# Two-layer hybrid encoder trunk: layer 2's first scale and shift loaded behind layer 1's experts, one more spare place, first copies reordered

## Chip, cores and metric

The kernel runs on one core of one Trainium2 chip. The metric is device time in microseconds (us) for one execution; lower is better. "Layer 1" is the first layer (index 0 in the code), "layer 2" the second (index 1).

## What is computed

256 tokens of width 1024 pass through two layers. Each layer is a mixer (layer 1: forgetting attention, layer 2: latent attention on keys and values that are computed once, between the layers) and a mixture of 16 experts with top-2 routing inside one group. Every sub-layer begins with an RMS norm and a shift and scale that come from a condition vector c, and ends with a gain from c:

```python
c_act = jax.nn.silu(c)
for layer in range(DEPTH):
    sh1, sc1, g1, sh2, sc2, g2 = jnp.split(c_act @ w_mod[layer] + b_mod[layer], 6, axis=-1)
    h = modulate(rmsnorm(x, norm_g), sh1, sc1)
    ...
    x = x + g1[:, None, :] * mix
    h = modulate(rmsnorm(x, ffn_norm_g[layer]), sh2, sc2)
    x = x + g2[:, None, :] * grouped_moe(h, ...)
    if layer == 0:
        shared_kv = mla_shared_kv(x, c_act, kv_norm_g, kv_w_mod, kv_b_mod, kv_w_down, ...)
return rmsnorm(x, final_norm_g)
```

All is float32. Every weight is read once from HBM, some 294 MB in all. `c_act @ w_mod` is a product of one row with a 1024 x 1024 block for each of the scales, shifts and gains: 4 MB to load, little to compute.

## The kernel before

**The stream of loads.** `plan` lists all weight loads in one order (lines 175 to 243), and SyncE's queue (SP) issues them in it as places come free, as far as the planner of the tile framework does not put one whose place is free ahead of one whose place is not. Most places are the ring `wp`: `NB` = 10 tiles of 1 MB. During the experts some loads go to spare places instead, made of tiles that lie idle then (`SPARE`, `SPAT`: the n-th entry of `SPAT[l]` names the expert load that goes to the n-th entry of `SPARE[l]`). `places` gives each later expert load the place of an earlier one. `give` opens a spare place, `drop` frees the place of the load at the head of the stream, `done` drops and then calls `mods`.

**Scales, shifts, gains.** They are entries `("mod", name, j)` of the same stream, four loads of 1 MB each (for the first scale and shift of layer 1 two halves of two loads, names in `HALVES`). `mods` (L323) works off those at the head of the stream. A name in `ONPE` is done on TensorE (L343): the column of c_act, spread to 32 columns, times the load, four products side by side. Any other name is done on VectorE (L349, L351): eight products over 128x1024 that add up in a tile `macc`, closed by short products with ones (L470). `finish_at[name]` then turns the row into columns: a copy out of PSUM (L476), a 4 KB DMA on GpSimd's queue (L482), and the bias and norm gain on VectorE (L483, L485); or, for a gain, spreads it over the partitions (L507, L509).

**Order of the instructions.** The planner of the tile framework orders each engine's instructions ahead of time, by its own idea of when operands and loads arrive; on the chip each engine then works strictly in that order. `tc.issue_after(i)` keeps what it encloses behind instruction `i` on `i`'s engine. `hold` names entries that `mods` leaves alone until they are released; `later` puts products behind a given instruction.

**Stages.** (1) Layer 1's input: norm, transposes, and the first group's products in two halves of the width (`turn_half`, `half_qk`, `half_v`, `half_f`). A weight is split on ScalarE and on VectorE or GpSimd into a high and a low part (`split`, L543, L544), and each product is three products (`mm3`, L548 to L550). (2) Attention over four groups of heads, then the output weight `a_w_o`. (3) `moe(0)`: router, routing on VectorE, gather of the tokens into 64 slots per expert (`fetch`, L895), then eight pairs of experts: gate and up products (`wide`, L925), down products (L1050), scatter products (L940, for the last pair L1076). Scale and shift of the attention between the layers (`sc_kv`, `sh_kv`) and layer 2's `sc1_1`, `sh1_1` are loaded ahead of the experts, the gain `g2_0` behind the first four expert loads. `sc1_1` is done on VectorE during the output weight, `sh1_1` on TensorE behind the router's products (L791 to L794). (4) `turn` (L574): norm, transposes (L583) and two sets of scaled parts (`leave`: L597, L603, L605, L606), `hk` for the keys and values with `sc_kv`, `sh_kv`, and `h2` for the queries with `sc1_1`, `sh1_1`; then products of `hk` with `kv_w_down` (`kvd`) and of `h2` with `b_w_dq` (`dq`). Layer 2's gain `g1_1` comes next in the stream and is done on VectorE. (5) Attention and output weight of layer 2, (6) `moe(1)`, (7) final norm.

Of the kernel before, what the change touches and what calls it, by code (L numbers as in the profile page):

```python
# [22 lines left out]
F32 = mybir.dt.float32  # L23
# [7 lines left out]
D = 1024  # L31
# [13 lines left out]
NEG = -1.0e30  # L45
NB = 10
HALVES = ('sc1_0a', 'sh1_0a', 'sc1_0b', 'sh1_0b')
ONPE = HALVES + ('sc2_0', 'sh_kv', 'sh1_1', 'g2_0', 'sc2_1', 'g2_1')
MB = 6
MP = (4, 0, 0, 0, 1, 1, 2, 1, 1, 2, 0, 0, 0, 0)  # L50
QA = (1, 0)
# [3 lines left out]
G2IN = 0  # L55
GAT = 4
LO = {'wf': 'V', 'wo0': 'VP', 'wo1': 'PVVV', 'in': 'PPPV', 'inv': 'P', 'kvd': 'VVPVPVPV', 'dq': 'PPVP', 'kvu': 'PV', 'uqr': 'VP', 'uq': 'P'}
SPAT = ((8, 9, 10, 11, 12, 13, 14), (3, 4, 5, 9, 10, 11, 12, 13, 14, 15))
KVF = 1
PVAT = 1  # L60
ORD = (1, 1, 0, 1, 2, 3)
# [13 lines left out]
def trunk_kernel(ctx, tc, A, out):  # L75
# [10 lines left out]
    def bank(i):  # L86
        return psp.tile([128, 512], F32, name=f"b{i}", tag=f"b{i}")
# [35 lines left out]
    class Pieces:  # L123
# [11 lines left out]
        def __getitem__(self, at):  # L135
            t, c = self.at[at[1]]
            return t[at[0], c + (at[2].start or 0):c + (at[2].stop or 512)]

    SPARE = {0: (("ka",) * 2, ("o8",), ("at",) * 4, ("at", "at", "v", "v"), ("wl",) * 4, ("wh",) * 4, ("x",)),
             1: (("yb", "yb", "g2"), ("macc",) * 2, ("ka",) * 2, ("o8",), ("at",) * 4, ("at", "at", "v", "v"), ("wl",) * 4,  # L140
                 ("g1", "ckvT"), ("wh",) * 4, ("x",))}
    AGAIN = (("at",) * 4, ("at", "at", "v", "v"), ("macc",) * 2, ("wl",) * 4, ("wh",) * 4, ("ka",) * 2)
# [50 lines left out]
    def in_half(j, c):  # L193
        return ("in", 0, j, c), win[:, 4 * c:4 * c + 4, j * D:j * D + 256]

    scb, shb = mod_half("sc1_0b", D + D // 2), mod_half("sh1_0b", D // 2)
    for it in (mod_half("sc1_0a", D) + mod_half("sh1_0a", 0)
               + [in_half(0, 0), scb[0], in_half(1, 0), scb[1], shb[0], in_half(2, 0), shb[1], (("wf", 0), wff[:, 0:4]),
                  (("wf", 1), wff[:, 4:8])]):
        plan(*it)  # L200
    main = [in_half(j, 1) for j in range(3)]
# [3 lines left out]
    wo = A["a_w_o"][0].rearrange("(k p) n -> p k n", p=128)  # L205
    for j in range(4):
        plan(("wo0", j), wo[:, 2 * j:2 * j + 2, :])
    side = (mod_unit("sc_kv", KVM, D) + mod_unit("sh_kv", KVM, 0)
            + mod_unit("sc1_1", W1, D) + mod_unit("sh1_1", W1, 0))
    for it in side:  # L210
        plan(*it)
    plan_moe(0, mod_unit("g2_0", W0, 5 * D))
    r = A["kv_w_down"].rearrange("(p k) n -> p k n", k=8)
    for j in range(2):
        plan(("kvd", j), r[:, 4 * j:4 * j + 4, :])
# [30 lines left out]
    state = {"issued": 0, "used": 0, "held": 0}  # L246
    macc = {}
    spare = []
    hold = {"sh1_1"}

    def issue():
        while state["issued"] < len(stream):
# [60 lines left out]
                            A["pack"][64 * c:64 * c + 64, ga0:ga0 + 8].rearrange("(q a) k -> q a k", a=16))  # L313

    def later(name, j):
        if name not in ("g2_0", "g2_1") or G2IN:
            return ExitStack()
        return behind(ORD[2 + j] if j < 4 else j)
# [4 lines left out]
    def mods():  # L323
        while state["used"] < len(stream) and stream[state["used"]][0][0] == "mod":
            key = stream[state["used"]][0]
            if key[1] in hold:
                return
            _, name, j = key
            w = get(key)
            if j == 0:  # L330
                macc[name] = bank(MB)[:, 0:128 if name in HALVES else 256] if name in ONPE else big.tile([128, D], F32, name="macc", bufs=2)
                if name in brows:
                    l, i = brows[name]
                    nc.gpsimd.dma_start(bcast[0:128:32, :],
                                        A["b_mod"][l, i * D:i * D + D].rearrange("(q n) -> q n", q=4))
            acc = macc[name]
            nk, n = (4, 128) if name in HALVES else (2, 256)
            for kk in range(nk):
                k = nk * j + kk
                if name in ONPE:  # L340
                    with later(name, j):
                        for q in range(4):
                            PE.matmul(acc[32 * q:32 * q + 32, :], cact[:, k:k + 1].to_broadcast([128, 32]),  # L343
                                      w[:, kk, n * q:n * q + n], start=k == 0, stop=k == 7)
                else:
                    at = state.get("rope") or state.get("turned")
                    with tc.issue_after(at) if at else ExitStack():
                        if k == 0:
                            V.tensor_scalar(acc, w[:, kk, :], cact[:, 0:1], None, op0=ALU.mult)  # L349
                        else:  # L350
                            V.scalar_tensor_tensor(acc, w[:, kk, :], cact[:, k:k + 1], acc,  # L351
                                                   op0=ALU.mult, op1=ALU.add)
            drop()
            if k == 7:
                if name in finish_at:
                    with later(name, 4):
                        finish_at.pop(name)()
# [216 lines left out]
    def turn(src, stride, nk, outs, banks):  # L574


        pss = {}
        for kk in range(0, nk, 2):
            ps = bank(banks[(kk // 2) % len(banks)])
            for k in (kk, kk + 1):  # L580
                for t in range(T):
                    o = (k - kk) * 256 + t * 128
                    PE.transpose(ps[:, o:o + 128], src[:, t, k::stride], ident)  # L583
            pss[kk] = ps.rearrange("p (a b) -> p a b", a=2)
            if len(outs) == 1:
                leave(pss, kk, *outs[0])
        if len(outs) > 1:
            for o in outs:
                for kk in range(0, nk, 2):
                    leave(pss, kk, *o)  # L590

    def leave(pss, kk, dst, G, sh, pair):
# [9 lines left out]
            else:  # L602
                SC.activation(hf[:, i], psv[:, i], AF.Identity, scale=G[:, k:k + 1], bias=sh[:, k:k + 1])  # L603
        if pair:
            SC.activation(d_[:, 0], hf, AF.Copy)  # L605
            at = (PL if kk % 4 else V).tensor_tensor(d_[:, 1], hf, d_[:, 0].bitcast(F32), op=ALU.subtract).ins  # L606
            if kk % 4 == 0:
                state["left"] = at
# [164 lines left out]
    def moe(l, G, sh, acc):  # L773
# [4 lines left out]
        for t in range(T):  # L778
            for c in range(2):
# [8 lines left out]
                for kk in range(4):  # L788
                    after[1] = PE.matmul(z[t], xT[:, kk, :], rwG[:, 4 * c + kk, :],
                                         start=c == 0 and kk == 0, stop=c == 1 and kk == 3).ins  # L790
        if hold:  # L791
            hold.clear()
            with tc.issue_after(after[1]):
                mods()  # L794
        give(l, "wh")
        rs = [rstd(slice(t, t + 1))[t] for t in range(T)]
        zz = wk.tile([128, T, E], F32, name="rzz", bufs=1)
# [207 lines left out]
        for i in range(E // 2):  # L1005
# [38 lines left out]
            for p, (c0, n) in enumerate(cols):  # L1044
# [3 lines left out]
                for k in range(4):  # L1048
                    for e in range(2):
                        at = PE.matmul(py[64 * e:64 * e + 64, 0:n], aT[:, k, 64 * e:64 * e + 64], ws[e][:, k, :],  # L1050
                                       start=k == 0, stop=k == 3).ins
                if i == OV - 1 and p == 1:
                    with tc.issue_after(at):
                        tc.mark_branch_hint_location(f"over{l}", "LikelyTaken", [mybir.EngineType.PE])
# [15 lines left out]
                if i == E // 2 - 1:  # L1070
# [2 lines left out]
                        x.new()  # L1073
                    for t in range(T):
                        for j, (pt, y_) in enumerate(parts_):
                            PE.matmul(acc[t, half][:, o:o + n], pt[:, t, :], y_, start=False,  # L1076
                                      stop=o + n == 512 and j == len(parts_) - 1)
                        if o + n == 512:
                            ch = slice(512 * half, 512 * half + 512)
                            if l == 0:  # L1080
# [1 line left out]
                            squares(t, half, None, acc[t, half])  # L1082
                    if l and o + n == 512:
                        gains(half, acc)


    for c, nm in enumerate("ab"):
# [65 lines left out]

    turn_half(0)
    half_qk(0, 0)
    half_qk(1, 0)
    half_v(0)
    half_f(0)
    turn_half(1)
    state["turned"] = state["left"]  # L1160
    half_f(1)
# [63 lines left out]
    xn = normalise()  # L1225
    hk = [big.tile([128, 2, 2, S], F32R, name="hk", tag=("qa", "ka")[i % 2], bufs=2) for i in range(4)]
    h2, h2p = parts("h2")
    turn(xn, 8, 8, [(hk, M["sc_kv"], M["sh_kv"], True), (h2p, M["sc1_1"], M["sh1_1"], True)], (0, 1, 2, 3))

    def rms_small(srcs, n, dst):  # L1230
        sq = sm.tile([128, len(srcs)], F32, name="sq")
# [247 lines left out]
```

## Time and profile before

| | us |
|---|---|
| three runs | 850.89, 847.19, 845.97 (median 847.19) |
| the profiled execution | 847.37 |
| its span, first to last instruction | 845.2 |
| TensorE (PE) busy | 759.6 (90%) |
| VectorE (DVE) busy | 374.7 (44%) |
| ScalarE (ACT) busy | 265.5 (31%) |
| GpSimd (POOL) busy | 169.5 (20%) |
| HBM | 294.32 MB read, mean 351 GB/s |

Busy times are of one profiled execution; the rows of a view count from the start of its span. Weight loads of TensorE (PEld) overlap its products, and the ends of products are modelled. A wait is put down to what ended it. In a timeline, the bracket behind a row tells how long the engine stood before it and what released it.

### The profile page before, as it was taken

What the parts mean: (1) busy time and instruction counts of PE and PEld (TensorE: products, weight loads), DVE (VectorE), ACT (ScalarE), POOL (GpSimd) and SP (SyncE); (2) the same over time, 40 slices, a digit from 0 to 9 for tenths busy, and PEclk for the clock granted to TensorE, in tenths of its full rate; (3) what the DMA queues carried; (4) which work ended last, traced back from release to release, by engine and by line L of the source; (5) the groups of instructions that cost most, each with busy time, mean ns of one, the idle gap of its engine ahead of it and who ended that gap; (6) DMA issues with size and microseconds to landing.
All of it is one profiled execution on the core that took longest, in us unless ns stands there. A gap on an engine that the chain in (4) does not pass through costs nothing.

```text
span 845.2 us, 11973 instructions
## 1 busy us (share of the span) xinstructions
PE 759.6 (90%) x4530; PEld 454.3 (54%) x4530; DVE 374.7 (44%) x838; ACT 265.5 (31%) x576; POOL 169.5 (20%) x155
## 2 busy tenths in 40 slices
PE   4788999988999999899886899899799999999985
PEld 3678789656335454343335677777544544445322
DVE  2279699876113211211128949865712311223112
ACT  2345556534111110110116565766411201111002
POOL 3446376321000000000005846421100000000000
PEclk9799999999999999999998999999799999999998
DMA  9999788799999999999998678977879999999993
GB/s 320 372 378 351 250 326 297 287 382 390 412 399 394 414 403 405 415 405 405 418 401 309 202 275 313 348 248 244 304 262 396 395 373 418 388 390 401 396 405 134
DMA packets 105960, 296.35 MB, mean 351 GB/s; under 512 B 8164, under 2 KB 27804, under 8 KB 93600
## 3 DMA queue, kind: packets, MB, share of 16 engines
q1 hardware_dynamic: 104976, 293.79, 92.0%
q10 hardware_dynamic: 288, 1.05, 0.3%
q8 instruction: 39, 0.64, 0.3%
q0 software_dynamic: 624, 0.60, 0.3%
q14 instruction: 33, 0.27, 0.1%
HBM read 294.32 MB, written 1.05 MB: 349 GB/s over the span
## 4 chain that ended last, share of the span: by engine, by line
issue 22%; PE 21%; DVE 8%; DMA 8%; ACT 2%; SPq 0%; POOLq 0%; POOL 0%; another core or an unknown queue 0%; ACTq 0%; DVEq 0%
DMA w<-in_exp_w_up_dram 7%; PE b L925 5%; PE b L1050 3%; PE b L548 2%; DVE macc L351 2%; PE b L549 2%; PE b L550 2%; PE b L895 1%; DVE wl L544 1%; DMA fg<-in_final_norm_g_dram 1%; PE b L940 1%; PE b L657 1%; PE b L343 1%; PE b L643 1%; PE b L619 1%
## 5 line engine op out<-in xcount | busy, mean ns | idle before, releaser
L925 PE MATMUL b<-w,XG 128*64 128x512 f32 x1024 | 234.3, 595 | 15.5 <-DMA w<-in_exp_w_up_dram 6.9
L544 POOL TENSOR_TENSOR wl<-w,wh 128x512 fp32r<-128x512 f32 (+3 forms) x90 | 132.8, 1490 | 331.8 <-DMA w<-in_b_w_dq_dram 218.3
L925 PEld LDWEIGHTS b<-w,XG 128*64 128x64 f32 x1024 | 80.7, 137 | 156.1 <-issue 125.5
L1050 PE MATMUL b<-w,aT 128*64 128x512 f32 (+1 forms) x528 | 121.8, 586 | 4.0 <-ACT aT L1038 4.0
L1025 DVE SCALAR_TENSOR_TENSOR act<-sg,rcs,b 128x512 f32<-128x512 f32 x16 | 12.0, 748 | 204.2 <-PE b L925 178.4
L543 ACT ACTIVATE wh<-w 128x512 fp32r<-128x512 f32 (+3 forms) x136 | 77.2, 588 | 80.0 <-PE b L549 28.8
L1050 PEld LDWEIGHTS b<-w,aT 128*64 128x64 f32 x528 | 39.4, 136 | 63.2 <-issue 51.3
L351 DVE SCALAR_TENSOR_TENSOR macc<-w,cact,macc 128x1024 f32<-128x1024 f32 x42 | 68.6, 1633 | 0.4
L1065 ACT ACTIVATE yh<-yb 128x512 fp32r<-128x512 f32 x31 | 19.5, 630 | 102.7 <-DVE yb L1063 102.7
L544 DVE TENSOR_TENSOR wl<-w,wh 128x512 fp32r<-128x512 f32 (+2 forms) x46 | 39.4, 864 | 20.4 <-ACT wh L543 20.3
L1063 DVE TENSOR_TENSOR yb<-b,g 128x512 f32<-128x512 f32 (+1 forms) x33 | 22.2, 674 | 58.5 <-PE b L1050 57.1
L565 POOL TENSOR_TENSOR rs<-rs,mhalf 128x1 f32<-128x1 f32 (+1 forms) x9 | 5.9, 652 | 199.4 <-DVE rs L564 199.3
L343 PE MATMUL b<-w,cact 128*32 128x256 f32 (+1 forms) x640 | 40.0, 368 | 6.2 <-DMA w<-in_w_mod_dram 6.0
L1014 ACT ACTIVATE sg<-b 128x512 f32<-128x512 f32 x16 | 9.6, 597 | 113.3 <-PE b L925 113.3
L1038 ACT ACTIVATE aT<-b 128x256 f32<-128x256 f32 x16 | 6.1, 384 | 124.1 <-PE b L1035 124.1
L895 PEld LDWEIGHTS b<-P,xs 128*128 128x128 f32 x256 | 35.9, 211 | 16.0 <-DVE XG L901 8.9
L548 PE MATMUL b<-h,wh 128*128 128x256 f32 (+1 forms) x136 | 41.1, 307 | 3.0 <-ACT h L605 2.2
L550 PE MATMUL b<-h,wl 128*128 128x256 f32 (+1 forms) x136 | 41.4, 306 | 1.2 <-POOL wl L544 0.9
L895 PE MATMUL b<-P,xs 128*128 128x256 f32 x256 | 40.9, 312 | 1.6 <-DVE P L860 1.6
L549 PE MATMUL b<-h,wh 128*128 128x256 f32 (+1 forms) x136 | 40.9, 302 | 0.0
L901 DVE TENSOR_SCALAR XG<-b,c_sc,c_sh 128x256 f32<-128x256 f32 x32 | 17.4, 543 | 36.6 <-ACT XG L903 36.4
L903 ACT ACTIVATE XG<-b,c_sh,c_sc 128x256 f32<-128x256 f32 x32 | 17.9, 560 | 46.9 <-PE b L895 46.9
(310 smaller groups left out, 1237.0 us busy)
## 6 DMA issues: line engine op xcount, KB each, us to landing
w<-in_exp_w_down_dram SPq DMA_DIRECT2D x50, 1024.0 KB, 14.8
w<-in_w_mod_dram SPq DMA_DIRECT2D x48, 1024.0 KB, 9.7
w<-in_exp_w_gate_dram SPq DMA_DIRECT2D x48, 1024.0 KB, 14.0
w<-in_exp_w_up_dram SPq DMA_DIRECT2D x48, 1024.0 KB, 15.1
w<-in_exp_w_gate_dram SPq DMA_DIRECT2D x42, 256.0 KB, 8.3
w<-in_exp_w_up_dram SPq DMA_DIRECT2D x40, 256.0 KB, 6.6
w<-in_a_w_in_dram SPq DMA_DIRECT2D x9, 1024.0 KB, 12.0
w<-in_kv_w_mod_dram SPq DMA_DIRECT2D x8, 1024.0 KB, 6.5
```

Of the source, the lines that this page charges most:

```text
L343: PE.matmul(acc[32 * q:32 * q + 32, :], cact[:, k:k + 1].to_broadcast([128, 32]), w[:, kk, n * q:n * q + n], start=k == 0, stop=k == 7)
L351: V.scalar_tensor_tensor(acc, w[:, kk, :], cact[:, k:k + 1], acc, op0=ALU.mult, op1=ALU.add)
L543: SC.activation(hi, src, AF.Copy)
L544: lo_eng.tensor_tensor(lo, src, hi.bitcast(F32), op=ALU.subtract)
L548: PE.matmul(ps, l[0], r_[0], start=start, stop=False)
L549: PE.matmul(ps, l[0], r_[1], start=False, stop=False)
L550: PE.matmul(ps, l[1], r_[0], start=False, stop=stop)
L895: at = PE.matmul(ps[:, 256 * kk:256 * kk + 256], xs[n % 2, n // 2][:, 128 * k:128 * k + 128], P[g][:, n // 2].rearrange("p e s -> p (e s)" ...
L925: last = PE.matmul(ps[64 * e:64 * e + 64, :], XG[i // 2, k // 4][:, k % 4, o:o + 64], ws[e][:, kk, :], start=k == 0, stop=k == 7).ins
L1050: at = PE.matmul(py[64 * e:64 * e + 64, 0:n], aT[:, k, 64 * e:64 * e + 64], ws[e][:, k, :], start=k == 0, stop=k == 3).ins
L1063: V.tensor_tensor(yb[:, 0:n], py[:, 0:n], M[f"g2_{l}"][:, cs_], op=ALU.mult)
L1065: SC.activation(yh[:, 0, cs_], yb, AF.Copy)
```

## The change

Four things change. `sc1_1` is done on TensorE, in PSUM bank 4. The eight loads of `sc1_1` and `sh1_1` stand behind all expert loads of layer 1 instead of ahead of them, and their products are placed by `later`: the first half of the scale behind the last down product of the layer, its second half and the shift's first load behind the last scatter product, the rest of the shift behind the last transpose of `turn`, which now works off what is held before it scales. The spare place (`ckvT`, `g2`) takes expert load 3 of layer 1. At the start, two halves of the scale and one of the shift are loaded ahead of the second input weight, the last half of the shift ahead of the third, and the second and third weights' work is kept behind ScalarE's last high part of the first half and behind the products of the shift's halves.

```diff
-ONPE = HALVES + ('sc2_0', 'sh_kv', 'sh1_1', 'g2_0', 'sc2_1', 'g2_1')
+ONPE = HALVES + ('sc1_1', 'sc2_0', 'sh_kv', 'sh1_1', 'g2_0', 'sc2_1', 'g2_1')
...
-SPAT = ((8, 9, 10, 11, 12, 13, 14), (3, 4, 5, 9, 10, 11, 12, 13, 14, 15))
+SPAT = ((3, 8, 9, 10, 11, 12, 13, 14), (3, 4, 5, 9, 10, 11, 12, 13, 14, 15))
...
-    SPARE = {0: (("ka",) * 2, ("o8",), ("at",) * 4, ("at", "at", "v", "v"), ("wl",) * 4, ("wh",) * 4, ("x",)),
+    SPARE = {0: (("ckvT", "g2"), ("ka",) * 2, ("o8",), ("at",) * 4, ("at", "at", "v", "v"), ("wl",) * 4, ("wh",) * 4, ("x",)),
...
-               + [in_half(0, 0), scb[0], in_half(1, 0), scb[1], shb[0], in_half(2, 0), shb[1], (("wf", 0), wff[:, 0:4]),
+               + [in_half(0, 0), scb[0], scb[1], shb[0], in_half(1, 0), shb[1], in_half(2, 0), (("wf", 0), wff[:, 0:4]),
...
-    side = (mod_unit("sc_kv", KVM, D) + mod_unit("sh_kv", KVM, 0)
-            + mod_unit("sc1_1", W1, D) + mod_unit("sh1_1", W1, 0))
-    for it in side:
+    for it in mod_unit("sc_kv", KVM, D) + mod_unit("sh_kv", KVM, 0):
         plan(*it)
     plan_moe(0, mod_unit("g2_0", W0, 5 * D))
+    for it in mod_unit("sc1_1", W1, D) + mod_unit("sh1_1", W1, 0):
+        plan(*it)
...
-    hold = {"sh1_1"}
+    hold = {"sc1_1", "sh1_1"}
+    tail = {}
...
     def later(name, j):
+        if name == "sc1_1":
+            return tc.issue_after(tail["product" if j < 2 else "scatter"])
+        if name == "sh1_1":
+            return tc.issue_after(tail["scatter" if j < 1 else "turn"])
...
-                macc[name] = bank(MB)[:, 0:128 if name in HALVES else 256] if name in ONPE else big.tile([128, D], F32, name="macc", bufs=2)
+                macc[name] = bank(4 if name == "sc1_1" else MB)[:, 0:128 if name in HALVES else 256] if name in ONPE else big.tile([128, D], F32, name="macc", bufs=2)
...
         if len(outs) > 1:
-            for o in outs:
+            hold.clear()
+            mods()
+            for d_, G, sh, pair in outs:
+                o = (d_, M[G], M[sh], pair)
                 for kk in range(0, nk, 2):
                     leave(pss, kk, *o)
...
-            SC.activation(d_[:, 0], hf, AF.Copy)
+            state["high"] = SC.activation(d_[:, 0], hf, AF.Copy).ins
...
-        if hold:
-            hold.clear()
-            with tc.issue_after(after[1]):
-                mods()
...
+        hold.discard("sc1_1")
+        mods()
...
     turn_half(0)
     half_qk(0, 0)
-    half_qk(1, 0)
-    half_v(0)
-    half_f(0)
+    with tc.issue_after(state["high"]), tc.issue_after(state["mod", "sh1_0b", 0]):
+        half_qk(1, 0)
+    with tc.issue_after(state["mod", "sh1_0b", 1]):
+        half_v(0)
+        half_f(0)
```

Left out above: where `tail["product"]`, `tail["scatter"]`, `tail["turn"]` and `state["mod", ...]` are noted (the last down product, scatter product, transpose and product so far), and `turn`'s call, which names its columns instead of passing them.

## Rows read from the trace of the kernel before

**Rows 1.** The page's busy times: engine, busy us, share of the span, instructions
```profile
PE 759.6 (90%) x4530; PEld 454.3 (54%) x4530; DVE 374.7 (44%) x838; ACT 265.5 (31%) x576; POOL 169.5 (20%) x155
```

**Rows 2.** Stages: from:to, us, busy of the engines, TensorE's clock, DMA share, GB/s
```profile
42.30:63.40 21.10, 16.91 (x171) 15.70 (x169) 16.66 (x18) 10.34 (x17) 10.15 (x7) 0.92 1.06 379
...
128.00:176.00 48.00, 43.42 (x281) 35.86 (x279) 43.57 (x79) 27.50 (x64) 24.39 (x17) 1.00 0.81 296
...
212.00:440.00 228.00, 212.36 (x1022) 91.21 (x1020) 44.88 (x94) 27.65 (x50) 0.80 (x2) 1.00 1.03 406
...
448.00:456.00 8.00, 5.93 (x31) 5.29 (x32) 5.26 (x13) 4.86 (x13) 2.62 (x3) 0.64 1.01 395
456.00:488.00 32.00, 26.41 (x150) 21.20 (x148) 31.88 (x40) 19.91 (x44) 29.40 (x22) 1.00 0.61 214
...
613.00:633.00 20.00, 20.00 (x111) 8.30 (x110) 2.84 (x8) 3.57 (x5) 0.00 (x0) 0.97 0.72 259
633.00:824.00 191.00, 184.88 (x878) 80.47 (x877) 40.89 (x82) 22.99 (x42) 0.61 (x1) 1.00 1.03 396
```

**Rows 3.** Timeline, start: VectorE, ScalarE and TensorE (start us, us, what, idle before)
```profile
21.57 0.16 DVE L497 COPY c_sh_0a<-b 128x4 f32<-128x4 f32 x1 [0.48 <-PE b L495]
...
25.46 1.15 ACT L543 ACTIVATE wh<-w 128x512 fp32r<-128x512 f32 x2 [3.88 <-DMA w<-in_a_w_in_dram]
26.52 1.00 ACT L603 ACTIVATE hf<-b,c_sh_0a,c_sc_0a 128x256 f32<-128x256 f32 x2
...
23.27 1.60 PE L343 MATMUL b<-w,cact 128*32 128x128 f32 x32 [1.73 <-DMA w<-in_w_mod_dram]
28.20 1.50 PE L343 MATMUL b<-w,cact 128*32 128x128 f32 x22 [3.33 <-DMA w<-in_w_mod_dram]
...
45.75 0.16 DVE L497 COPY c_sh_0b<-b 128x4 f32<-128x4 f32 x1 [0.48 <-PE b L495]
...
47.88 0.95 PE L548 MATMUL b<-h,wh 128*96 128x256 f32 x3 [2.16 <-ACT h L605]
```

**Rows 4.** VectorE's products (page, whole kernel); timelines ahead of layer 1's experts
```profile
L351 DVE SCALAR_TENSOR_TENSOR macc<-w,cact,macc 128x1024 f32<-128x1024 f32 x42 | 68.6, 1633 | 0.4
...
175.35 1.85 PE L517 MATMUL b<-pack,c_sh 128*128 128x16 f32 x15 [2.73 <-DVE c_sh L483]
...
182.38 1.28 DVE L351 SCALAR_TENSOR_TENSOR macc<-w,cact,macc 128x1024 f32<-128x1024 f32 x1
...
196.41 3.66 PE L343 MATMUL b<-w,cact 128*32 128x256 f32 x64
...
208.87 1.08 PE L925 MATMUL b<-w,XG 128*64 128x512 f32 x4
```

**Rows 5.** Chain of waits through layer 1's experts: start us, us, what
```profile
364.85 3.65 PE b L925 x14
...
406.40 19.85 DMA w<-in_exp_w_up_dram
```

**Rows 6.** SyncE's queue, timeline at 422; DMA issues of 395 to 445, median to landing
```profile
422.26 6.58 SPq L263 DMA_DIRECT2D w<-in_kv_w_down_dram  x2
...
w<-in_kv_w_down_dram SPq DMA_DIRECT2D x2, 576.0 KB, 13.9
```

**Rows 7.** Timelines behind layer 1's experts: TensorE, ScalarE, VectorE
```profile
450.07 3.68 PE L583 MATMUL b<-idc,xn 128*128 128x128 f32 x16 [3.14 <-DVE xn L571]
453.73 0.40 PE L548 MATMUL b<-wh,hk 128*128 128x288 f32 x1
...
461.41 0.52 PE L548 MATMUL b<-wh,h 128*128 128x512 f32 x2
...
456.71 1.01 ACT L603 ACTIVATE hf<-b,c_sh,c_sc 128x256 f32<-128x256 f32 x2
...
457.95 1.33 DVE L349 TENSOR_SCALAR macc<-w,cact 128x1024 f32<-128x1024 f32 x1
```

**Rows 8.** DMA issues of 186 to 215: a small copy on GpSimd's queue, us to landing
```profile
c_sh<-mrows POOLq DMA_DIRECT2D x1, 4.0 KB, 6.0
```

More of the change, by code (lines that the diff above doesn't have):

```diff
@@ L342, in mods @@
                         for q in range(4):
-                            PE.matmul(acc[32 * q:32 * q + 32, :], cact[:, k:k + 1].to_broadcast([128, 32]),
-                                      w[:, kk, n * q:n * q + n], start=k == 0, stop=k == 7)
+                            state[key] = PE.matmul(acc[32 * q:32 * q + 32, :], cact[:, k:k + 1].to_broadcast([128, 32]),
+                                                   w[:, kk, n * q:n * q + n], start=k == 0, stop=k == 7).ins
                 else:
@@ L582, in turn @@
                     o = (k - kk) * 256 + t * 128
-                    PE.transpose(ps[:, o:o + 128], src[:, t, k::stride], ident)
+                    tail["turn"] = PE.transpose(ps[:, o:o + 128], src[:, t, k::stride], ident).ins
             pss[kk] = ps.rearrange("p (a b) -> p a b", a=2)
@@ L1051, in moe @@
                                        start=k == 0, stop=k == 3).ins
+                tail["product"] = at
                 if i == OV - 1 and p == 1:
@@ L1075, in moe @@
                         for j, (pt, y_) in enumerate(parts_):
-                            PE.matmul(acc[t, half][:, o:o + n], pt[:, t, :], y_, start=False,
-                                      stop=o + n == 512 and j == len(parts_) - 1)
+                            tail["scatter"] = PE.matmul(acc[t, half][:, o:o + n], pt[:, t, :], y_, start=False,
+                                                        stop=o + n == 512 and j == len(parts_) - 1).ins
                         if o + n == 512:
@@ L1227, in trunk_kernel @@
     h2, h2p = parts("h2")
-    turn(xn, 8, 8, [(hk, M["sc_kv"], M["sh_kv"], True), (h2p, M["sc1_1"], M["sh1_1"], True)], (0, 1, 2, 3))
+    turn(xn, 8, 8, [(hk, "sc_kv", "sh_kv", True), (h2p, "sc1_1", "sh1_1", True)], (0, 1, 2, 3))
     def rms_small(srcs, n, dst):
```

## The prediction

> **What bounds the kernel now.** I read the page's busy shares first, then the stage table, then the timelines at the two places the change touches, and last the chain of waits through layer 1's experts. TensorE is busy 90% of the span, so no stage has much air, but the stages differ [rows 1]. In the stage table the reader should look at the DMA share and at VectorE. From 212 to 440 us (layer 1's experts) the DMA share is 1.03 at 406 GB/s, while TensorE is busy 212.36 of 228.00 us, which leaves 15.6 us idle. Before it, 128 to 176, the DMA share is 0.81. Behind it, 456 to 488, it is 0.61, and there VectorE is busy 31.88 of 32.00 us [rows 2]. So the transfers have nothing to spare inside the experts and have room on both sides of them. The chain says the same: it runs through loads of an up weight issued 18 to 20 us ahead (19.85 from 406.40 on) and through the 3.65 us of products that waited for them [rows 5]. Layer 2's experts end in the same way (1.03 from 633 to 824, only 0.72 just before) [rows 2]: there the places are full when they start, so whatever time is won ahead of them arrives at the end whole.
>
> Two smaller places. At the start ScalarE waits 3.88 us for the second input weight, with the first half's scaling queued behind it: its columns are in place at 21.7, the scaling runs at 26.52. The second half's columns come at 45.75 and its products start at 47.88 [rows 3]. Late in layer 1's attention TensorE stands 2.73 us for a VectorE addition, and a VectorE product of 1.28 us stands directly ahead of an addition to x [rows 4].
>
> **The change part by part.** The sum is made against the profiled execution: span 845.2, own time 847.37, which is 0.18 above the median of 847.19.
>
> *First copies.* No transfer is added; two half scales and a shift go ahead of one input weight, and a shift ahead of another. The stream brings about 1 MB in 2.5 to 2.8 us here (23.27, 25.46, 28.20 are landings) [rows 3], so the last half shift moves from about 35 to about 33 us. The new order also puts the second weight's split behind the first half's scaling on ScalarE. That scaling then starts at about 21.7 instead of 26.5. On TensorE the last half shift's products are no longer queued behind three weights' products, so its columns are there near 38 instead of 45.75, and the second half starts near 41 instead of 47.88. That is up to 7 us; the input weights of the next groups come one per 2.6 us and cap it. None at all is the other end. I take 5.
>
> *The scale as products.* VectorE loses one L349 and seven L351 products, 8 x 1.633 = 13.1 us [rows 4], and TensorE the few L470 sums that close them. Most of it lies in shadow. On the path lie the 1.28 us at 182.38 and, of the 2.73 us for which TensorE waited at 175.35, about 2.2, since such a product stood ahead of the addition it waited for: 0 to 3.5, I take 2.5. TensorE gets as much as the shift costs it, 64 records in 3.66 us [rows 4], behind the experts. Cover: the wait for kv_w_down below. Without that cover it would be 3.7.
>
> *The shift moved.* Its 3.66 us at 196.41 end before a wait for VectorE of the routing (TensorE's next product is later), so taking them away gains 0. At the new place they have the same cover.
>
> *One more place.* One expert load more lies in SBUF when the experts start: with ten ring places (4 gain loads, 6 expert loads) and eight others, 14 of 96. The gain's write to that tile has to wait for the products of the load that lay there; in order they come before it anyway: 0.
>
> *The eight loads.* They leave the stretch before the experts and come behind them on SP's queue, ahead of kv_w_down, b_w_dq, kv_w_up and layer 2's first gain, each of which comes eight loads later in the stream. Experts first: products start at 208.87 now [rows 4], so at 208.9 - 5 - 2.5 = 201.4. By then all places are full, and the first comes free 3.65 us later, at 205.05 [rows 5]. From there to the landing of kv_w_down the stream carries 82 expert loads (86.0 MB), the eight (8.4 MB) and 1.2 MB: 95.6 MB at 406 GB/s [rows 2] are 235.4 us. With about 2 us until the first transfer runs (0 to 4: a 4 KB copy alone takes 6.0 from issue to landing [rows 8]) it lands at 442.4. Today it is issued at 422.26 and lands 13.9 later by the median, around 436 to 442, and its products start only at 453.73 [rows 6, 7]. So it lands no earlier than now, and **what the change spends is the cushion of some 14 us** between that landing and its use.
>
> TensorE is not the limit: its last expert products move by 7.5 plus up to 15.6, to 420 or so. x follows them, and kv_w_down is then what comes last. Split and first product: 443.9 against 453.73, 9.8 earlier. The other branch is the columns of layer 2's shift: last load 442.4 - 2.9 = 439.5, a quarter of its products 0.9, row copy 0.4, the small copy through POOL's queue 6.0 [rows 8], an addition 0.2: 447.0 against 456.71 [rows 7], 9.7 earlier. b_w_dq's products hang on it. I take 9.7.
>
> *Given back there.* With the cushion gone, engines that work in order meet loads they used to find in place; VectorE's products of g1_1 (457.95) stand between the scalings of this stage [rows 7]. The two small copies also cost POOL an issue each. Bounds 0 and 7; I take 1.2, near the small end, because b_w_dq (3.1 MB right behind kv_w_down) lands from about 444 to 450, the first load some seven us ahead of its first product.
>
> Sum: 9.7 - 1.2 = 8.5 earlier, and that passes through the rest: **847.37 - 8.5 = 838.9, less 0.18: 838.7**. Its own range is 834 to 843.
>
> **A rule weighed against it.** In 448 to 456 TensorE's granted clock is 0.64, part of it on the 1.2 GHz level, and before that the engine had stood 3.14 us for VectorE [rows 2, 7]. The Trainium skill, "TensorE: Matmul & The Clock Gate", section "Why this matters for your kernels", tells to leave no idle gaps between bursts of matmuls, or the clock falls back; that speaks against letting TensorE wait for kv_w_down, and for the products that now lie in the gap. Trace and rule agree on the direction. The sum has neither gain nor loss for it; the loss is a rival.
>
> **The rivals.**
> *The start doesn't pass on* (the change does not do there what it says): the next input weights come no earlier than now, and the DMA share is 1.06 as late as 42 to 63 us [rows 2]. Then 5 us fall away: 843.7. For it: landings set the pace there. Against: ScalarE's and TensorE's queue order, not a landing, set 26.52 and 45.75.
> *More*: the start gives 7, VectorE 3.5, nothing is given back, and VectorE, freed of the gain's products until b_w_dq is through (13 of its 31.88 us), shortens that stage by some 3: 831.
> *The clock* falls in the wait ahead of kv_w_down: a stretch like that of 448 to 456, 8 us at 0.64, loses 2.9: 841.6.
> *Slower*: VectorE stands in the seam. The start does not pass on, so kv_w_down lands at 447.4, and the first load of g1_1, 5.2 MB behind, at 460.3. If VectorE's order holds its product between the first and second scaling as now, VectorE stands from about 453, some 7.5 us; and if the last of the four loads comes late because its place does, about 3 more: 847.37 - 4.7 + 7.5 + 3 = 853. It decides from where VectorE's waits for w_mod between 445 and 475 come to about 10 us together. For it: nothing in the order forbids it. Against: the order is made by a planner that has the loads' times in view.
>
> **How the numbers follow.** Forecast 0.47, start lost 0.18, more 0.16, clock 0.07, slower 0.12. A measurement can tell about 0.5%, 4.2 us, from no change. Faster by more: 0.44 of the forecast, all of "more", most of "clock", a little of "start lost": 0.68. Within: 0.20. Slower: 0.12. The range reaches to "more" (with some beyond 831) and to the milder half of "slower", with the 0 to 4 us of the first transfer in it: 827 to 850.
>
> **What would show it.** In the profile after: ScalarE's first scaling near 22 and the second half's products near 41; the wait at L517 gone or short; expert products from about 201; DMA share 1.0 from then past 440; the last expert products 15 us or more earlier; then TensorE waiting for kv_w_down or for a column, with the first b_w_dq product near 452 (461.41 now [rows 7]); the rest a plain shift. Wrong, if expert products start no earlier than 206, if the DMA share falls below 0.95 inside the experts, or if VectorE waits for w_mod in the seam.

## The result, and the profile after

The changed kernel is slower: 861.14 us median of 4 runs (859.87 to 862.62) against 848.28 of 4 (845.97 to 850.89), a ratio of 1.0152 with a 95% interval of 1.0124 to 1.0180. The forecast was 838.7, with a range of 827 to 850. The profiled execution (span 858.1, own time 859.87) shows where it goes.

The page's busy times after, against [rows 1]:

```profile
PE 767.1 (89%) x4586; PEld 464.0 (54%) x4586; DVE 359.7 (42%) x830; ACT 266.2 (31%) x576; POOL 158.5 (18%) x155
```

Work changed as meant: VectorE has 15 us less, TensorE 7.5 more. The stage table after, columns as in [rows 2], and below it the row of the kernel before for 212 to 300:

```profile
42.30:63.40 21.10, 15.45 (x108) 14.60 (x107) 18.83 (x19) 12.40 (x21) 11.07 (x8) 0.88 1.06 378
128.00:176.00 48.00, 45.71 (x292) 37.26 (x291) 37.62 (x83) 28.06 (x66) 21.89 (x16) 1.00 0.82 302
196.00:206.00 10.00, 6.94 (x45) 5.93 (x45) 7.98 (x44) 2.30 (x4) 0.00 (x0) 0.54 1.02 404
206.00:212.00 6.00, 6.00 (x32) 2.60 (x34) 0.99 (x4) 1.59 (x4) 0.00 (x0) 1.00 0.65 225
212.00:300.00 88.00, 86.85 (x416) 41.20 (x414) 18.12 (x39) 11.72 (x20) 0.55 (x1) 1.00 0.93 353
300.00:440.00 140.00, 129.03 (x614) 54.24 (x610) 29.17 (x56) 16.25 (x32) 0.00 (x0) 1.00 1.03 408
456.00:470.00 14.00, 8.35 (x45) 6.54 (x44) 6.41 (x19) 6.90 (x14) 6.75 (x7) 0.87 1.04 388
470.00:479.00 9.00, 0.14 (x1) 0.14 (x1) 8.83 (x12) 2.98 (x6) 0.00 (x0) 0.50 0.88 338
```

```profile
212.00:300.00 88.00, 85.28 (x450) 37.02 (x448) 18.76 (x43) 11.23 (x19) 0.55 (x1) 1.00 1.03 405
```

Two stretches stand out. From 206 to 300 the DMA share is low (0.65, then 0.93 at 353 GB/s, where the kernel before has 1.03 and 405 from 212 to 300), although this is where the stream should have run full. From 470 to 479 TensorE does nothing (0.14 of 9.00), VectorE is busy 8.83, and the clock is at its lower level, 1.2 GHz (0.50).

**Where the stream falls behind.** The first line of the DMA view from the start to 196, to 300, to 440, to 470 and to 640 us: what had moved by then. Before:

```profile
DMA packets 30730, 64.90 MB, mean 331 GB/s; under 512 B 2764, under 2 KB 15208, under 8 KB 30316
...
DMA packets 42525, 106.80 MB, mean 356 GB/s; under 512 B 3767, under 2 KB 16227, under 8 KB 39319
...
DMA packets 58162, 163.78 MB, mean 372 GB/s; under 512 B 4655, under 2 KB 17115, under 8 KB 50830
...
DMA packets 61411, 172.70 MB, mean 367 GB/s; under 512 B 4878, under 2 KB 18362, under 8 KB 54076
...
DMA packets 78823, 220.76 MB, mean 345 GB/s; under 512 B 6052, under 2 KB 23644, under 8 KB 70112
```

After:

```profile
DMA packets 30352, 64.66 MB, mean 330 GB/s; under 512 B 2796, under 2 KB 15244, under 8 KB 29584
...
DMA packets 41740, 101.12 MB, mean 337 GB/s; under 512 B 3640, under 2 KB 16092, under 8 KB 38643
...
DMA packets 56916, 158.28 MB, mean 360 GB/s; under 512 B 4511, under 2 KB 16963, under 8 KB 49712
...
DMA packets 60626, 170.19 MB, mean 362 GB/s; under 512 B 4834, under 2 KB 18318, under 8 KB 53418
...
DMA packets 76617, 215.15 MB, mean 336 GB/s; under 512 B 5956, under 2 KB 23548, under 8 KB 68116
```

Until 196 the two are level. At 300 the changed kernel is 5.68 MB behind, 14 us at 406 GB/s, and at 440 still 5.50 MB. Behind the experts it makes up more than half of that: at 470 it is 2.51 MB behind. At 640, early in layer 2's experts, it is 5.61 MB behind again; TensorE, which frees the places, is some 14 us late by then. So the lag at 300 is not by itself the 12.9 us by which the end comes late (spans). What the lag does is to bring kv_w_down late; where the 12.9 us arise is read in the seam below. SyncE's queue after, where the lag begins, in the timeline:

```profile
196.06 0.33 SPq L264 DMA_DIRECT2D w<-in_exp_w_gate_dram  x1
206.01 9.70 SPq L264 DMA_DIRECT2D w<-in_exp_w_up_dram  x4
```

And in the waits of 196 to 300 (us in total, times, longest), after:

```profile
SPq L264 <- PE b L929: 34.6, 10, 8.3
...
SPq L264 <- PE b L348: 5.3, 1, 5.3
```

And before:

```profile
SPq L263 <- PE b L925: 26.1, 9, 7.4
```

The queue issues nothing from 196.4 to 206.0. Loads that are under way keep the transfers busy until 206 (share 1.02); then they run short (0.65). Of that stand 3.6 us are put down to a count that the queue reads from the routing (L949), 5.3 to a product of a gain (L348), which frees a place. The reading is that every place is full at 196, since TensorE works off no load from 194.2 to 204.7, and that from then on the queue can issue only as TensorE frees places; TensorE has no air left to do that faster (86.85 of 88.00 us busy). The wait alone doesn't show this, since the queue of the kernel before waits for products too; the share does. An up weight lands 7.0 us after its issue (216 to 300), where it took 12.7 before; but e8_four below has 7.1 at a share of 1.01, so this time is no measure of the loss.

**The seam.** Timelines after, behind layer 1's experts: SyncE, TensorE, ScalarE, GpSimd, VectorE. They answer to [rows 6, 7].

```profile
435.26 2.08 SPq L264 DMA_DIRECT2D w<-in_kv_w_down_dram  x2
...
442.49 3.13 PE L588 MATMUL b<-idc,xn 128*128 128x128 f32 x16 [2.14 <-DVE xn L576]
445.55 5.43 PE L348 MATMUL b<-w,cact 128*32 128x256 f32 x80
454.40 0.61 PE L553 MATMUL b<-wh,hk 128*128 128x288 f32 x1 [3.42 <-ACT hk L613]
...
478.86 0.79 PE L553 MATMUL b<-wh,h 128*128 128x512 f32 x1 [9.72 <-ACT h L613]
...
447.55 0.38 ACT L481 ACTIVATE mrows<-b 128x256 f32<-128x256 f32 x1 [6.33 <-PE b L348]
450.92 1.44 ACT L548 ACTIVATE wh<-w 128x288 fp32r<-128x288 f32 x4 [2.99 <-DMA w<-in_kv_w_down_dram]
452.27 0.36 ACT L481 ACTIVATE mrows<-b 128x256 f32<-128x256 f32 x1
...
476.48 1.48 ACT L611 ACTIVATE hf<-b,c_sh,c_sc 128x256 f32<-128x256 f32 x3 [5.80 <-DVE c_sh L488]
...
452.92 0.69 POOL L487 DMA_DIRECT2D c_sh<-mrows  x1
...
466.28 0.19 DVE L1271 COPY kr<-b 128x32 f32<-128x32 f32 x1 [3.46 <-PE b L555]
...
469.62 0.75 DVE L354 TENSOR_SCALAR macc<-w,cact 128x1024 f32<-128x1024 f32 x1
...
471.12 5.25 DVE L356 SCALAR_TENSOR_TENSOR macc<-w,cact,macc 128x1024 f32<-128x1024 f32 x4
476.28 0.16 DVE L488 TENSOR_TENSOR c_sh<-c_sh,pack 128x8 f32<-128x8 f32 x1
```

The transposes come 7.6 us earlier than before. But kv_w_down's first load lands at 450.9, where ScalarE's split of it had waited 2.99 us (in the kernel before the split ran at 438.55). So the cushion in front of its use took up nearly all of that: its first product is at 454.40, 0.7 late. From there on more is lost. kv_w_down's products take 12.2 us, to 466.63, where 7.8 us sufficed; ScalarE's scalings for them stand behind that split. Then VectorE: the shift's column is issued at 452.92 and lands 5.7 later, at 458.6. Its addition (L488) runs at 476.28, because VectorE's order has it behind the rotary copies, which wait for the last kv_w_down product (3.46), and behind five products of layer 2's first gain. ScalarE waits for the addition, and the first b_w_dq product comes at 478.86 for 461.41. The last one ends at 500.09 for 486.07, 14.0 late, and the rest is a plain shift: the first product of layer 2's experts is 14.3 late (631.34), the end 12.9.

### The profile page after: what moved, and what is told of

The parts are those of the page before. It is cut to its first block, busy times and chain, and to the rows that moved or that the text cites. A ratio compares the mean times of both kernels' runs of the same rounds, so it can differ in the third digit from the quotient of the medians.

```text
span 858.1 us, 12081 instructions
## 1 busy us (share of the span) xinstructions
PE 767.1 (89%) x4586; PEld 464.0 (54%) x4586; DVE 359.7 (42%) x830; ACT 266.2 (31%) x576; POOL 158.5 (18%) x155
## 5 line engine op out<-in xcount | busy, mean ns | idle before, releaser
L929 PE MATMUL b<-w,XG 128*64 128x512 f32 x1024 | 234.7, 595 | 11.5 <-DMA w<-in_exp_w_up_dram 6.2
L929 PEld LDWEIGHTS b<-w,XG 128*64 128x64 f32 x1024 | 84.7, 137 | 148.1 <-issue 123.8
L549 POOL TENSOR_TENSOR wl<-w,wh 128x512 fp32r<-128x512 f32 (+3 forms) x90 | 121.5, 1362 | 140.2 <-ACT wh L548 131.5
L356 DVE SCALAR_TENSOR_TENSOR macc<-w,cact,macc 128x1024 f32<-128x1024 f32 x35 | 52.1, 1489 | 0.4
L348 PE MATMUL b<-w,cact 128*32 128x256 f32 (+1 forms) x704 | 47.0, 375 | 4.8 <-DMA w<-in_w_mod_dram 4.3
L553 PE MATMUL b<-wh,h 128*128 128x256 f32 (+1 forms) x96 | 28.3, 322 | 9.7 <-ACT h L613 9.7
L348 PEld LDWEIGHTS b<-w,cact 128*32 128x32 f32 x704 | 22.0, 119 | 24.0 <-issue 9.2
## 6 DMA issues: line engine op xcount, KB each, us to landing
w<-in_w_mod_dram SPq DMA_DIRECT2D x48, 1024.0 KB, 12.2
w<-in_exp_w_up_dram SPq DMA_DIRECT2D x48, 1024.0 KB, 11.5
```

What stands on the lines that cost most here:

```text
L348: state[key] = PE.matmul(acc[32 * q:32 * q + 32, :], cact[:, k:k + 1].to_broadcast([128, 32]), w[:, kk, n * q:n * q + n], start=k == 0, st ...
L549: lo_eng.tensor_tensor(lo, src, hi.bitcast(F32), op=ALU.subtract)
L553: PE.matmul(ps, l[0], r_[0], start=start, stop=False)
L929: last = PE.matmul(ps[64 * e:64 * e + 64, :], XG[i // 2, k // 4][:, k % 4, o:o + 64], ws[e][:, kk, :], start=k == 0, stop=k == 7).ins
```

## The experiments

Ratios are against the kernel before, run beside them. Its medians were 849.13 (for e1, e2, e3, e7), 848.88 (e4, e6, e8, e9), 847.93 (e5, e10, e11) and 848.75 (e12).

**1. VectorE's order.** e1_order keeps the rotary copies, b_w_dq's splits and the gain's products behind the addition; e2_gain_only the gain's products alone.

```diff
-        V.tensor_tensor(r_, r_, bias, op=ALU.add)
+        state["col", name] = V.tensor_tensor(r_, r_, bias, op=ALU.add).ins
...
+                    if name == "g1_1":
+                        at = state["col", "sh1_1"]
...
-        V.tensor_copy(kr[:, t, :], pd[t][:, KVR:KVR + ROPE])
+        with tc.issue_after(state["col", "sh1_1"]):
+            V.tensor_copy(kr[:, t, :], pd[t][:, KVR:KVR + ROPE])
...
-            ws = split(get(("dq", k // 2))[:, k % 2, 512 * j:512 * j + n], "dq")
+            with tc.issue_after(state["col", "sh1_1"]):
+                ws = split(get(("dq", k // 2))[:, k % 2, 512 * j:512 * j + n], "dq")
```

> The changed kernel with one thing more: VectorE's rotary copies, its splits of b_w_dq and its products of layer 2's first gain are kept behind the addition that ends the shift's column. Theory 'order' (VectorE does the addition at 476.28 although its column landed near 458.6, because other work stands ahead of it): the addition comes near 463, the first b_w_dq product near 469 instead of 478.86, no half clock before it, time 847 to 851. Rival 'loads' (the eight loads and kv_w_down behind them land too late, whatever the order): the first b_w_dq product no earlier than 475, time 857 to 861.

> The changed kernel with only the products of layer 2's first gain kept behind the addition of the shift's column; the rotary copies stay ahead of it. Theory 'order': the addition comes near 469, behind the rotary copies that wait for kv_w_down's last product, the first b_w_dq product near 472, time 852 to 855, between the changed kernel and the run with everything behind it. Rival 'loads': 857 to 861.

Measured: e1 857.42 (1.0090, 1.0065 to 1.0116), e2 856.15 (1.0067, 1.0045 to 1.0090). The timelines of e1, VectorE, ScalarE, TensorE:

```profile
464.77 0.16 DVE L490 TENSOR_TENSOR c_sh<-c_sh,pack 128x8 f32<-128x8 f32 x1
...
467.99 1.14 ACT L550 ACTIVATE wh<-w 128x512 fp32r<-128x512 f32 x2 [2.44 <-PE b L557]
469.04 1.46 ACT L613 ACTIVATE hf<-b,c_sh,c_sc 128x256 f32<-128x256 f32 x3
...
472.23 0.70 PE L555 MATMUL b<-wh,h 128*128 128x512 f32 x1 [3.54 <-ACT h L615]
```

The addition comes 11.5 us earlier, the first b_w_dq product 6.6, the end 2.5 by the spans (858.1 and 855.6), 3.7 by the medians and 5.3 by the ratios. Behind the addition the next wait is ScalarE's own order: two splits that wait for a product stand ahead of the scaling. The two runs can't be told apart. Both are clear of the changed kernel (1.0124 to 1.0180), so VectorE's order is real: worth 3.7 to 5.3 us in e1, 5.0 to 7.2 in e2, by medians and by ratios. "order" had the addition and the clock (1.00 from 463 to 472), but put both times too low; "loads" had e1's time and missed its b_w_dq product and, by 0.9 us, e2's time. Most of the loss stays.

**2. kv_w_down ahead of the eight loads** (e7_kvd_first, on top of e1; the shift's parts are then scaled behind kv_w_down's products, and the scale's products use another PSUM bank, both not shown here):

```diff
-    for it in mod_unit("sc1_1", W1, D) + mod_unit("sh1_1", W1, 0):
-        plan(*it)
     r = A["kv_w_down"].rearrange("(p k) n -> p k n", k=8)
     for j in range(2):
         plan(("kvd", j), r[:, 4 * j:4 * j + 4, :])
+    for it in mod_unit("sc1_1", W1, D) + mod_unit("sh1_1", W1, 0):
+        plan(*it)
```

> The order of VectorE as in the first run of this set, and kv_w_down's two loads ahead of the eight instead of behind them (the shift's parts are scaled behind kv_w_down's products; the scale uses PSUM bank 7). Theory 'order': kv_w_down's products start near 446 instead of 454.4, but the shift's column waits for the same eight loads, so the first b_w_dq product stays within 3 us of the first run's and the time within 3 us of it. Rival 'loads': what is late is kv_w_down, so the time falls by 6 to 8 below the first run's.

Measured 851.05 (1.0032, 1.0013 to 1.0050). What it had moved by 300 us, and TensorE and VectorE in the timeline:

```profile
DMA packets 41616, 100.87 MB, mean 336 GB/s; under 512 B 3639, under 2 KB 16091, under 8 KB 38519
...
458.25 1.93 PE L348 MATMUL b<-w,cact 128*32 128x256 f32 x32
471.03 0.80 PE L555 MATMUL b<-wh,h 128*128 128x512 f32 x1 [10.85 <-ACT h L613]
...
466.64 0.17 DVE L490 TENSOR_TENSOR c_sh<-c_sh,pack 128x8 f32<-128x8 f32 x1 [8.37 <-DMA c_sh<-mrows]
```

At 300 its stream is as far behind as the changed kernel's (100.87 MB for 101.12), and yet it ends 1.9 us (medians) to 4.0 us (spans) behind the kernel before. So the lag costs that little if kv_w_down comes first and VectorE's order fits: given the lag, most of the loss comes by the order of loads and instructions behind the experts. What the eight loads would cost without the lag no run shows. Its first kv_w_down product is at 449.17, its first b_w_dq product at 471.03, 1.2 before e1's, because the column is late again: its last products stand directly behind kv_w_down's on TensorE (458.25). The time still fell by 6.4. Half of that is there when layer 2's experts start (625.06, 3.3 before e1's 628.35), the other half arises inside them; by 640 it has moved 217.62 MB, e1 216.30. Each theory is right on one count; why the experts gain is not settled.

**3. Half the move** (e8_four, with e1's order; e9_four_no_spare also without the new place). The scale's four loads go back ahead of the experts, its products behind the router's (the lines for the products are left out below).

```diff
-    for it in mod_unit("sc_kv", KVM, D) + mod_unit("sh_kv", KVM, 0):
+    for it in mod_unit("sc_kv", KVM, D) + mod_unit("sh_kv", KVM, 0) + mod_unit("sc1_1", W1, D):
         plan(*it)
...
-    for it in mod_unit("sc1_1", W1, D) + mod_unit("sh1_1", W1, 0):
+    for it in mod_unit("sh1_1", W1, 0):
         plan(*it)
```

> Half of the move: the scale's four loads stay ahead of the experts (its products on TensorE behind the router's), only the shift's four go behind them; VectorE's order as in the run with everything behind the addition. Theory 'places' (eight loads ahead of time fill every place at 196, so the queue stands still and what was gained on it is lost: 0.93 and 0.92 of the DMA share from 200 to 300): with four the share stays near 1.03 from 212 to 300, the last expert load lands near 429 to 432, kv_w_down near 441 to 443 instead of 452.2, the first b_w_dq product near 460 to 463, time 841 to 846. Rival 'tail' (any load behind the experts makes the shift's column late by its landing, product, copy and small transfer, some 9 us): first b_w_dq product no earlier than 467, time 848 to 852.

> As the run before, without the new spare place. Theory 'places': one place fewer costs nothing where the queue no longer stands still, and the input weights land 2.5 earlier at the start: within 2 us of the run before. If the spare place is what carries the gain: 2 to 3 us slower.

Measured: e8 847.20 (0.9981, 0.9966 to 0.9996), e9 845.71 (0.9968, 0.9952 to 0.9984). e8's stretch of 212 to 300 in the stage table:

```profile
212.00:300.00 88.00, 85.25 (x448) 37.24 (x446) 18.11 (x40) 11.83 (x20) 0.55 (x1) 1.00 1.01 396
```

What it had moved by 300 us:

```profile
DMA packets 42709, 105.01 MB, mean 350 GB/s; under 512 B 3732, under 2 KB 16188, under 8 KB 39612
```

Its first b_w_dq product in TensorE's timeline:

```profile
461.53 0.80 PE L553 MATMUL b<-wh,h 128*128 128x512 f32 x1 [3.84 <-ACT h L613]
```

The share is back at 1.01, 3.9 of the 5.68 MB are back, b_w_dq starts as before the change, and 10.2 us of e1's time are gone. "places" called it, but for the time, which it put at 841 to 846. The run does two things at once, though: the stream keeps its rate, and four loads fewer stand ahead of kv_w_down. e7, where the rate is not back, has 6.4 of the 10.2 us, so the rate alone is not shown to be worth more than the remaining 4 us.

**4. The first copies and the new place** on the kernel before: e4_copies has the reorder alone, e5_copies_spare the place too; e3_no_spare is the changed kernel without the place. Place and reorder are the edits of the change itself.

> The kernel before with the reordered first copies alone. Theory 'the spare's load ate it' (the expert load for the new place goes out at 22.5 and takes 2.5 us from the input weights): alone the copies bring the experts' first product from 208.87 to 206 to 207 and the time to 845 to 847. Rival 'the landings set the pace anyway': experts' start within 0.5 of 208.87, time 847 to 849.

> The kernel before with the reordered first copies and the new spare place, nothing moved. Theory 'the spare's load ate it': the expert load for the new place goes out among the first copies, the fifth input weight lands near 44.6 instead of 42.2, and 2 to 3 of the copies' 4.3 us are gone: 846.5 to 848. Rival 'an expert load more in place when the experts start is worth its 2.6 us': 842 to 844.

> The changed kernel without the new spare place. Theory 'its load goes out at once' (the expert load for that place is issued at 22.5, when landings set the pace, and pushes the input weights back by 2.5 us): without it the fifth input weight lands near 42 instead of 44.57, the experts start near 205 instead of 207.57, time 1 to 3 less than the changed kernel's. Rival 'places' (the stream waits for places while the experts run, 0.92 of the DMA share from 230 to 300): with one place fewer kv_w_down lands about 2.6 later and the time is 1 to 3 more.

Measured: e4 844.57 (0.9953, 0.9933 to 0.9974), e5 847.16 (0.9982, 0.9964 to 0.9999), e3 858.24 (1.0091, 1.0061 to 1.0121). Timelines of e5, SyncE and ScalarE, with the place:

```profile
22.20 3.62 SPq L275 DMA_DIRECT2D w<-in_exp_w_gate_dram  x2
...
37.86 2.00 ACT L543 ACTIVATE wh<-w 128x512 fp32r<-128x512 f32 x4 [6.28 <-DMA w<-in_a_w_in_dram]
```

And of e4, ScalarE and TensorE, without it:

```profile
35.28 1.15 ACT L543 ACTIVATE wh<-w 128x512 fp32r<-128x512 f32 x2 [3.52 <-DMA w<-in_a_w_in_dram]
...
203.23 1.07 PE L925 MATMUL b<-w,XG 128*64 128x512 f32 x2
```

The tile of the new place is free from the start, so its expert load goes out at 22.20, among the first copies, and the third input weight comes 2.6 us later. The reorder alone is worth 4.3 us; with the place 0.8 is left. Without the place the changed kernel is 2.9 faster by the medians, though the spans differ by 0.4 only; "places", which put it slower, is not borne out. But its experts start at 207.41 and not near 205: something else holds them in the changed kernel (see below).

**5. The scale on TensorE at its old place** (e6_scale_pe: the kernel before with `sc1_1` added to `ONPE` and to `hold`).

> The kernel before with the scale done on TensorE instead of VectorE, at its old place in the stream, behind the router's products like the shift. If the whole of 208.87 - 207.57 and the earlier router (186.91 for 190.66) came from VectorE's freed 13 us: router near 187, experts' first product 205 to 207. If transfers bound the experts from then on, the last expert load still lands near 437 and the time stays within 2 us of before (847 to 850); if TensorE's start does, the time falls by 2 to 4.

Measured 850.04 (1.0002, 0.9985 to 1.0019). The wait at L517 [rows 4] is gone there too, the router starts 0.6 earlier and the experts 1.5 (207.41), and nothing reaches the end.

**6. Towards a better kernel.** e10_column_early is e9 with the shift's products behind the last down and scatter products; e11_gain_late is e10 with the gain's products behind the scaling of the shift's parts; e12_copies_gain_late has that and the reorder on the kernel before.

```diff
-            return tc.issue_after(tail["scatter" if j < 1 else "turn"])
+            return tc.issue_after(tail["product" if j < 2 else "scatter"])
...
+    state["h2"] = state["left"]
...
+                    if name == "g1_1":
+                        at = state["h2"]
```

> The run with four loads behind the experts and no new spare place, with one thing more: the shift's products stand behind the last down product and the last scatter product instead of behind the transposes. If what is left of the loss in the seam is the column's tail (products held behind the transposes, and ScalarE's row copy ahead of the scaling for kv_w_down): kv_w_down's first product near 446 instead of 449.64, the first b_w_dq product near 457, time 841 to 843.5. If transfers hold it: within 1.5 us of 845.7.

> As the run before, and the products of layer 2's first gain stand on VectorE behind the scaling of the shift's parts. If VectorE is what holds the stage up (31.88 of 32.00 us busy in the kernel before): b_w_dq's products end 2 to 4 us earlier, time 839 to 842. If the gain's four places are missed by the loads behind it: no gain, or 1 to 2 us more.

> The kernel before with the reordered first copies, and the products of layer 2's first gain on VectorE behind the scaling of the shift's parts; nothing moved, no new spare place. If what the run with four loads behind the experts won over the kernel before (843.73 for 847.93) came from the first copies and the gain's place alone, this run has it too: 841 to 844. If the moved half carries part of it: no better than the first copies alone, 844 to 846.

Measured: e10 846.54 (0.9973, 0.9954 to 0.9992), e11 843.73 (0.9941, 0.9919 to 0.9964), e12 847.93 (0.9993, 0.9973 to 1.0014). e10 missed: the planner left the last load's products behind the transposes all the same (445.57), and ScalarE's row copy at 447.57, which waits for them, stayed ahead of the first scaling, so the tail was not tested. e11 is the fastest run, but its interval lies over e4's: no version with a moved load is shown to beat the reorder alone. e10's interval lies over e11's as well, so the gain's later place is not shown to help there. e12 missed both ranges. e4, which leaves the gain where it was, is faster by 3.4 us, with intervals that just touch; why is open.

## Why the prediction was wrong

*First copies* (5 taken). The first scaling came at 21.45 (21.7 forecast), the second half's columns at 42.71, 3.0 earlier (38 forecast, 7.75 earlier). Alone the reorder gives 4.3 us, and the experts' first product comes at 203.23, 5.6 earlier. So the size is right, but with columns that came less than half as much earlier it was in part luck. In the change the experts start at 207.57, only 1.3 earlier; the next term says why.

*The shift moved* (0 taken). Wrong. Its products used to fill a part of TensorE's wait for the routing. TensorE's timelines there, after, and then of e4, where they still do:

```profile
198.20 0.19 PE L852 MATMUL b<-rmask,strictb 128*128 128x32 bf16 x1 [4.04 <-DVE rmask L848]
...
199.31 5.46 PE L899 MATMUL b<-P,xs 128*128 128x256 f32 x24 [0.86 <-DVE P L864]
...
198.03 2.89 PE L895 MATMUL b<-P,xs 128*128 128x256 f32 x22 [0.79 <-DVE P L860]
```

The gather of the tokens starts 4.0 earlier than in the kernel before (199.31 for 203.35), so up to there the start did pass on. But TensorE had stood 4.04 us, the granted clock was 0.50 from 196 to 204 (the 1.2 GHz level; e4 has 1.00 from 196 to 206), and 24 gather products took 5.46 us, where 22 took 2.89 in e4. e3, without the new place, shows the same (5.46 us, 207.41). The whole gather took 1.1 us more than in the kernel before, whose clock falls in part too, and 2.3 more than in e4. With other products in that wait e8 had 1.00 there, but e9 0.67, so filling it doesn't always keep the clock.

*One more place* (0 taken). Wrong too: it asked when the place must be written again, not when its load goes out. It costs 2.6 us (844.57 to 847.16, intervals that just overlap) where landings set the pace.

*The scale as products* (2.5 taken). The wait it was read from is gone, but alone it gives 0 (e6).

*The eight loads* (9.7 taken, with the shift's column). This is the first of the two steps that decide the miss: "By then all places are full", and "from there ... the stream carries ... 95.6 MB at 406 GB/s". The restart was right, 206.01 for 205.05. The rate was not: the stream carried 225 GB/s from 206 to 212 and 353 from 212 to 300, and kv_w_down landed at 450.9 and not at 442.4. Those 8.5 us leave 1.2 of the 9.7. The reason read from the rows is that a stream whose places are all full runs at the pace at which products free them. The 406 was read from a kernel whose stream stands eight loads less far ahead of TensorE when the experts start. [rows 2] had 212 to 440 and 128 to 176, but not the 36 us between, where the loads came from. e8 fits: with half of them left there the share is 1.01. More places for eight loads were not tried.

*Given back* (1.2 taken, at most 7). This is the second step that failed, and the larger one of the two. With 1.2 us of gain left at the landing, the last b_w_dq product ends 14.0 late: 15.2 us were given back. Between the first kv_w_down product and the first b_w_dq product 7.7 us [rows 7] became 24.5. e1 takes 3.1 us off the end of the stage by VectorE's order, e7 another 2.7 by the order of the loads; the rest is not split up. The "slower" rival had the engine, VectorE, and the direction (853), but not the cause: VectorE did not wait for w_mod there, it did the gain's products and the rotary copies while a finished column lay behind them. Its argument against itself, that the planner has the loads' times in view, fell: the order was written out ahead of time and did not fit.

Of the three signs of being wrong that the prediction names, two came: the experts start later than 206, and the DMA share falls below 0.95 inside them. The last expert products came 7.6 us earlier, where 15 or more were forecast.

*The clock* fell in the seam as well, with that wait. TensorE had stood 9.72 us ahead of 478.86, the granted clock was 0.50 in 470 to 479, and the first b_w_dq product took 0.79 us, where two took 0.52 before [rows 7]. The Trainium skill, "TensorE: Matmul & The Clock Gate", section "Why this matters for your kernels", warns of idle gaps between bursts; the trace agrees.

Put as a chain of kernels, each against the kernel before (ratios; a step is uncertain by about 0.002 to 0.004, and the steps add up because it is a chain; another order of the steps would share them out otherwise):

| step | edit | change of the ratio |
|---|---|---|
| before to e4 | first copies in order | -0.0047 |
| e4 to e5 | new place | +0.0029 |
| e5 to e8 | scale on TensorE, four loads moved, order as in e1 | -0.0001 |
| e8 to e7 | the scale's four loads moved too, all eight behind kv_w_down | +0.0051 |
| e7 to e1 | the eight ahead of kv_w_down, e7's two other edits taken back | +0.0058 |
| e1 to the change | VectorE's order as the planner made it | +0.0062 |
| sum | | +0.0152 |

## What to carry to other kernels

Before loads are moved behind a stretch, ask what the queue does where they were: if the places fill there, what was taken out is not gained; here it became standstill and then a slower stream. Ask also what stands behind them in the queue and is needed first: kv_w_down did, and putting it ahead of them gave back 6.4 us. A new buffer that is free from the start sends its load at once, so look at what that load pushes back. And when a short instruction becomes the last to be ready, look at what stands ahead of it on its in-order engine, and on the next one. Work that seems free to move because it ends before a wait may be what keeps TensorE's clock up in that wait.

## What was not expected of the hardware

A 4 KB copy between two tiles in SBUF took 5.7 us from issue to landing here, near the 6.0 that the prediction had taken [rows 8]; but it depends on what else moves. From the DMA issues of the changed kernel:

```profile
c_sc_kv<-mrows POOLq DMA_DIRECT2D x1, 4.0 KB, 2.2
...
c_sh<-mrows POOLq DMA_DIRECT2D x1, 4.0 KB, 5.7
```

The first was issued at 183.53, when the stream paused (DMA share 0.41 from 183.5 to 185.8), the second at 452.92, at a share of 1.01. The Trainium skill, "DMA: Bandwidth & Descriptors", section "Anatomy of one DMA — SWDGE (gpsimd) path", gives a fixed cost of about 2.0 us; the first copy agrees. Beside 1 MB loads at a share of 1.0 a column costs nearly three times that.
